# Turning the head outputs of the second half on VectorE, 32x32 blocks at a time, with the blocks moved by DMA

## The chip, the cores and the metric

The kernel runs on one core of a Trainium2 chip. The metric is the device time of one launch in microseconds (us). The core has five engines that run their own instruction streams and meet at semaphores: TensorE (PE, the matrix products, with its weight loads shown as PEld), VectorE (DVE), ScalarE (ACT), GpSimd (POOL) and SyncE (SP, which here only issues DMAs). On-chip memory (SBUF) has 128 partitions; PE writes into eight banks of PSUM, which DVE and ACT read.

## The reference

A hybrid encoder trunk of one layer over a sequence of 2048 tokens and 1024 features, in fp32:

```python
xn = rmsnorm(x, norm1_g[l])
z = xn @ w_in[l]
u_pool, zq, zf, zi, zo, zg = jnp.split(z, splits, axis=-1)
gates = jax.nn.sigmoid(zg + b_gate[l]).reshape(B, S, N_BRANCHES, D_MODEL)
ya = pool_mixer(u_pool, pool_w[l], pool_scale[l]) @ w_pa[l]
yb = hgrn2_mixer(zq, zf, zi, zo, lower_bounds[l], hgrn_norm_g[l]) @ w_pb[l]
merged = gates[:, :, 0] * ya + gates[:, :, 1] * yb
x = x + merged @ w_o[l]
x = x + conv_glu_ffn(rmsnorm(x, norm2_g[l]), w_up[l], conv_w[l], conv_b[l], w_down[l])
```

`hgrn2_mixer` is a gated linear recurrence with four heads of 128 features. What matters here is its end, where `o` is what the recurrence put out, `norm_g` a weight of 128 features that all heads share, and `zo` the output gate:

```python
o = o * lax.rsqrt(jnp.mean(o * o, axis=-1, keepdims=True) + EPS) * norm_g.astype(jnp.float32)
o = o * jax.nn.silu(heads(zo))
return o.reshape(B, S, HGRN_WIDTH).astype(zq.dtype)
```

The product with `w_pb` follows, which sums over the features.

## The kernel before

The sequence is cut into four blocks of 512 tokens (`TB`), and the program runs over two halves of two blocks: mixer (`mixer(b0)`, b0 = 0 and 2), then FFN. The large products are split into seven smaller ones (P1 to P7, in the manner of Strassen, on sums of quarters), and each is three matmuls in fp32r: every fp32 operand is a high part (a rounded copy, by ScalarE) and a low part (the difference, by VectorE). This is done by `split` (line 718 on, in the profile L724 and L725) for activations and by `Stream.convert` for the weights, whose rows in the profile are `ops<-raw` on ACT (L260) and DVE (L266). The weights are loaded by SP into eight buffers `raw` (`N_RAW`, L207) and turned into operands in six buffers `ops` (`N_OPS`).

The order is that of the code as it is written out, by generators: every sixth large matmul (`MM_PER_TICK`) calls `tick`, which advances the stream of weights and steps each open task; a task's `yield n` puts off its next piece by n ticks. All engines work through their own list in that order, as a scheduler in the framework lays it. `slots` is a pool of 73 SBUF buffers of 128x512 that all activations share, `banks` the eight PSUM banks: a tile that takes a buffer waits for the last reader of the tile before.

While the input projection runs (units `fr`, `gr` and others, seven products each, all of line 158 on PE), three runners (`N_RUN`) work through the eight pairs of block and head of the half (`hgrn_task(b, h, ...)`). Such a task starts when the projection has brought its `q` and `f` (L1316), goes through a chain of small DVE operations (L1175 to L1247) and PE products `pl` (L1155, L1227), the state (`pv`, `po`), and ends so:

- `ot` (L1295): four DVE operations, `po` by the reciprocal root and the output gate `z`; token on the partitions, feature along the row, 128 tokens in each of four pieces;
- four ticks later `pt` (L1301): four PE transposes of 128x128 fp32 into a bank, so that features come onto the partitions;
- `oh` (L1303): ScalarE copies the bank and multiplies by the norm's weight (`col(o_hg)`, one value for each partition);
- `spill` (L1120): ScalarE's queue stores the tile to a DRAM tile `od[b, h]` of 128x512, 256 KB.

Later in the same mixer, `o_task` fetches the eight tiles `od` into `oT` (SP, L1125), waits for a place in the program (`O_PLACE`), and splits each into `oTs` (high and low). These are the moving operands of the matmuls of `branch("pb", ...)`, the product with `w_pb` (`pb<-oTs_...` on PE), first for the lower block's chains, then for both in turn.

The first half (blocks 0 and 1) does the same.

Of the kernel before, what the change touches and what calls it, by code (L numbers as in the profile page):

```python
# [11 lines left out]
F32 = mybir.dt.float32  # L12
F32R = mybir.dt.float32r
U8 = mybir.dt.uint8
AF = mybir.ActivationFunctionType
ALU = mybir.AluOpType
AX = mybir.AxisListType

P = 128
# [3 lines left out]
HEADS = 4  # L23
# [6 lines left out]
TB = 512  # L30
NT = TB // P
SB = 1024
# [39 lines left out]
O_PLACE = 17  # L72
FIN_WAIT = 4
AHEAD = 3
GK = 32
NG = 4
ADD_LAG = 3
# [12 lines left out]
def tile_trunk(  # L90
# [17 lines left out]
    pe, act, dve, pool, sp = nc.tensor, nc.scalar, nc.vector, nc.gpsimd, nc.sync  # L108
# [7 lines left out]
    dram = ctx.enter_context(tc.tile_pool(name="dram", bufs=1, space=bass.MemoryType.DRAM))  # L116
    banks = ctx.enter_context(tc.tile_pool(name="banks", bufs=8, space=bass.MemoryType.PSUM))

    def slot(name, cols=TB, dt=F32):
        return slots.tile([P, cols], dt, tag="s", name=name, padded_shape=[P, 528])  # L120

    def bank(name, cols=512):
        return banks.tile([P, cols], F32, tag="b", name=name, padded_shape=[P, 512])

    def f32(ap):
        return ap.bitcast(F32)
# [513 lines left out]
    o_n1, o_n2, o_bg, o_ps, o_lb, o_hg, o_cb, o_cw = offs  # L640
# [8 lines left out]
    def col(o):  # L649
        return cols[:, o : o + 1]  # L650
# [19 lines left out]
    def setup_task():  # L670
# [8 lines left out]
        for key, x, off, w in keys:  # L679
# [8 lines left out]
                               channel_multiplier=-1)  # L688
            m8 = const.tile([P, GK // 2], U8, tag=f"m{key}", name=f"m{key}")
            yield 2  # L690
            for g in range(NG):
                r = slice(g * GK, g * GK + GK)
                pool.tensor_copy(m8[r], mf[r, g * GK // 2 : (g + 1) * GK // 2])
            masks[key] = m8.rearrange("p (b h) -> p b h", h=x)
        m8 = const.tile([P, GK], U8, tag="md", name="md")
        for g in range(NG):
            r = slice(g * GK, g * GK + GK)
            ins = pool.tensor_copy(m8[r], ident[r, r])
# [19 lines left out]
    def split(src, name, on_pool=False):  # L718
        hi = slot(name + "h", TB, F32R)
        lo = slot(name + "l", TB, F32R)  # L720
        if on_pool:
            up = pool.tensor_scalar(hi, src, 1.0, 0.0, ALU.mult, ALU.add)
        else:
            up = act.copy(hi, src)  # L724
        low = dve.tensor_tensor(lo, src, f32(hi), ALU.subtract)  # L725
        last_split[0] = up, low
        return hi, lo
# [395 lines left out]
    def fetch(d, name, eng=sp):  # L1123
        t = slot(name)
        eng.dma_start(t, d)  # L1125
        return t


    def hgrn_task(b, h, d, q, vd, zd, od):
        def head_of(src, key):  # L1130
            t = slot(f"{key}{b}_{h}")
            sp.dma_start(t.rearrange("p (c v) -> p c v", c=NT), src[:, :, h * P : (h + 1) * P])
            return t
# [8 lines left out]
        qv, dv, av = (t.rearrange("p (c x) -> p c x", c=NT) for t in (q, d, att))  # L1142
        ac = av[:, :, P - GK : P]

# [4 lines left out]
        def products(hh, qm):  # L1149
            x = GK // 2  # L1150
            pa_ = bank(f"pl{b}_{h}_{hh}", NT * 3 * x)
            ps = pa_.rearrange("p (c x) -> p c x", c=NT)
            for c in range(NT):
                for g in range(NG):
                    ins = pe.matmul(ps[g * GK : g * GK + GK, c],  # L1155
                                    ks[:, c * P + g * GK : c * P + g * GK + GK],
                                    qm[:, c, :, g * x : g * x + x], start=True, stop=True)
                    if not (c or g):
                        in_turn(ins)
            return ps  # L1160
# [16 lines left out]
        dve.tensor_tensor(qo, qm[:, :, 2], de, ALU.mult)  # L1177
        yield AHEAD
        ps = products(1, qm)
# [9 lines left out]
        for hh in (2, 8, 32):  # L1189
# [19 lines left out]
            dve.tensor_tensor(q2, f1, d5[:, :, :, 0, 0:1].to_broadcast(full), ALU.mult)  # L1209
            yield AHEAD  # L1210
            if hh < GK:
                x = GK // 2
# [80 lines left out]
        ot = slot(f"ot{b}_{h}")  # L1293
        for c in range(NT):
            dve.scalar_tensor_tensor(ot[:, c * P : (c + 1) * P], po[:, c * P : (c + 1) * P],  # L1295
                                     r[:, c : c + 1], zt[:, c * P : (c + 1) * P],
                                     ALU.mult, ALU.mult)
        yield 4
        pt = bank(f"pt{b}_{h}")
        for c in range(NT):  # L1300
            pe.transpose(pt[:, c * P : (c + 1) * P], ot[:, c * P : (c + 1) * P], ident)  # L1301
        t = slot(f"oh{b}_{h}")
# [131 lines left out]
    def add_forms(two, forms, k, name, store=lambda p, t: None, sums=True, pin=lambda i: None,  # L1434
                  eng=pool):

        def comb(p, x0, x1, op):
            if (p, k) in forms or x0 is None or x1 is None:
                return
            t = slot(f"{name}_{p}_{k}")  # L1440
            pin(eng.tensor_tensor(t, x0, x1, op))  # L1441
            forms[p, k] = t
            store(p, t)

        for p, at in (("P1", (1, 0)), ("P2", (1, 1)), ("P4", (0, 1))):
            if (p, k) not in forms and at in two:
                forms[p, k] = two[at]
                store(p, two[at])
        if not sums:
            return  # L1450
        comb("P7", two.get((1, 0)), two.get((0, 0)), ALU.subtract)
        comb("P5", two.get((0, 0)), two.get((0, 1)), ALU.subtract)
        comb("P6", forms.get(("P5", k)), two.get((1, 0)), ALU.subtract)
        comb("P3", forms.get(("P6", k)), two.get((1, 1)), ALU.add)
# [84 lines left out]
    def mixer(b0, forms, late):  # L1539
# [4 lines left out]
        md, od, gd = {}, {}, {}  # L1544
# [11 lines left out]
        def runner():  # L1556
            while taken[0] < 2 * HEADS:
                if queue:
                    taken[0] += 1
                    yield from hgrn_task(*queue.pop(0))  # L1560
                else:
                    yield 1
# [124 lines left out]
        oT = {}  # L1687
# [70 lines left out]
        def evac_b(m, hf, g, ps):  # L1758
            gated(g, hf, g, ps)
            dve.tensor_tensor(y[m, hf], y[m, hf], g, ALU.add)  # L1760
            if m >= KD // 2 and hf:
                k = m - KD // 2
                two = {(h, r): y[k + r * (KD // 2), h] for h in range(2) for r in range(2)}
                add_forms(two, yf, k, f"yf{b0}", eng=dve)

        def o_task():
            t = {}
            for hf in range(2):
                for g in range(HEADS):
                    while (b0 + hf, g) not in od:  # L1770
                        yield 1
                    t[hf, g] = fetch(od[b0 + hf, g], f"oT{b0 + hf}_{g}")
            while place[0] < O_PLACE:
                yield 1
            for hf in range(2):
                for g in range(HEADS):
                    oT[hf, g] = split(t[hf, g], f"oTs{b0 + hf}_{g}")
                    yield 2

        otask = []  # L1780
        for d in range(2):
            units = [Unit(f"pa{b0}_{2 * d + e}", "pa", emit_a(2 * d + e)) for e in range(2)]
            for p in ORDER:
                place[0] += 1
                if (d, p) == (1, "P1"):
                    otask.append(Task(o_task()))
                for s_, hf in {"P6": ((1, 1),), "P5": ((0, 0),), "P7": ((1, 0),),
                               "P2": ((0, 1),)}.get(p, ()):
                    for e in range(2):
                        gate(0, 2 * d + e + KD // 2 * s_, hf)  # L1790
                while len(pf[FORM[p]]) < 2:
                    place[0] += 1
                    mtask.step()
                w = stream.get("pa")
                for e in range(2):
                    units[e].products(p, pf, pf[FORM[p]], w[:, :, e * 256 : e * 256 + 256])
                    units[e].after(p)
                stream.used(1)
# [279 lines left out]
    for b in range(0, SEQ // TB, 2):  # L2078
        forms, task, late = nxt
        if b:  # L2080
            join(task)
        forms, task, late = mixer(b, forms, late)
        join(task)
        nxt = ffn(b, forms, late)
# [51 lines left out]
```

## Time and profile before

| what | value |
|---|---|
| device time, median of 3 runs | 2461.87 us (2461.87 to 2462.55) |
| the profiled execution's own time | 2461.48 us |
| its span in the trace | 2459.8 us |
| mean granted clock of PE | 0.999 |
| HBM read and written | 403.55 MB, 200.81 MB |
| PE transposes `pt` of all 16 pairs | 64, of which 32 in the second half |

The span is what the instructions of the core cover; the device time has 1.7 us around it. The projection of the second half, with the heads' tasks in it, lies from about 1380 to 1660 us, the `pa` and `pb` products of that half follow, and then `w_o` and the FFN. In a timeline, a row is start, duration, engine, line, operation, the tile written, the tiles read, shapes and count; what stands in brackets at its end is the idle time of that engine ahead of it and what ended it. Matmuls are pipelined, so a duration there is longer than the distance to the next one's start. In a row of waits stand the sum in us, the count and the longest.

### The profile page before, as it was taken

What the parts mean: (1) busy time and instruction counts of PE and PEld (TensorE: products, weight loads), DVE (VectorE), ACT (ScalarE), POOL (GpSimd) and SP (SyncE); (2) the same over time, 40 slices, a digit from 0 to 9 for tenths busy, and PEclk for the clock granted to TensorE, in tenths of its full rate; (3) what the DMA queues carried; (4) which work ended last, traced back from release to release, by engine and by line L of the source; (5) the groups of instructions that cost most, each with busy time, mean ns of one, the idle gap of its engine ahead of it and who ended that gap; (6) DMA issues with size and microseconds to landing.
All of it is one profiled execution on the core that took longest, in us unless ns stands there. A gap on an engine that the chain in (4) does not pass through costs nothing.

```text
span 2459.8 us, 37972 instructions
## 1 busy us (share of the span) xinstructions
PE 2439.1 (99%) x12624; PEld 1979.3 (80%) x12624; DVE 1903.0 (77%) x3294; ACT 1232.0 (50%) x2372; POOL 750.7 (31%) x1068
## 2 busy tenths in 40 slices
PE   9999999999999999999999999999999999999998
PEld 7887777788888888888888888888888888888887
DVE  7777776997998778876586667768889987878755
ACT  6545544435555445555544555542465554445534
POOL 4343353403354334451210101112033332335310
PEclk9999999999999999999999999999999999999999
DMA  8989888977888779899784443478333444447852
GB/s 283 312 218 277 237 220 238 329 221 245 206 251 242 225 226 240 269 364 321 237 285 153 136 127 122 154 237 306 112 129 129 150 156 134 145 144 260 306 165 99
DMA packets 272612, 529.29 MB, mean 215 GB/s; under 512 B 28640, under 2 KB 49248, under 8 KB 272096
## 3 DMA queue, kind: packets, MB, share of 16 engines
q1 hardware_dynamic: 204560, 348.47, 42.4%
q0 software_dynamic: 42880, 113.27, 18.1%
q10 hardware_dynamic: 24976, 65.13, 7.6%
q8 instruction: 99, 1.62, 0.3%
q14 instruction: 97, 0.79, 0.1%
HBM read 403.55 MB, written 200.81 MB: 246 GB/s over the span
## 4 chain that ended last, share of the span: by engine, by line
PE 92%; DVE 3%; DMA 2%; ACT 1%; issue 1%; POOL 0%; SPq 0%; ACTq 0%; DVEq 0%; POOLq 0%
PE dn_P L158 17%; PE up_Z L158 15%; PE up_X L158 10%; PE up_V L158 10%; PE wo_P L158 6%; PE gr_V L158 3%; PE pb L158 3%; PE gr_X L158 3%; PE io_Z L158 2%; PE io_V L158 2%; PE gr_W L158 2%; PE gr_Y L158 2%; PE fr_X L158 1%; PE gr_Z L158 1%; PE fr_V L158 1%; PE ur_X L158 1%
## 5 line engine op out<-in xcount | busy, mean ns | idle before, releaser
L260 ACT CAST ops<-raw 128x512 fp32r<-128x512 f32 x802 | 493.4, 620 | 784.8 <-PE dn_P L158 161.5
L266 DVE TENSOR_TENSOR ops<-raw,ops 128x512 fp32r<-128x512 f32 x774 | 571.4, 743 | 240.9 <-ACT ops L260 232.6
L1872 DVE SCALAR_TENSOR_TENSOR e<-h,cols,e 128x512 f32<-128x512 f32 x176 | 142.9, 817 | 30.3 <-ACT e L1870 26.9
L1870 ACT ACTIVATE e<-h,cols 128x512 f32<-128x512 f32 x176 | 142.2, 814 | 25.3 <-DVE h L1316 18.9
L1875 DVE SCALAR_TENSOR_TENSOR e<-h,cols,e 128x512 f32<-128x512 f32 x176 | 133.9, 770 | 2.5
L1125 POOL DMA_DIRECT2D g_P<-dg_P x154 | 83.0, 541 | 171.8 <-PE dn_P L158 133.0
L1441 POOL TENSOR_TENSOR gf_P<-e,e 128x512 f32<-128x512 f32 x44 | 61.1, 1390 | 149.5 <-DVE e L1881 85.8
L1441 POOL TENSOR_TENSOR gf_P<-gf_P,e 128x512 f32<-128x512 f32 x44 | 58.2, 1322 | 74.1 <-DVE e L1881 71.6
L501 POOL TENSOR_TENSOR raw<-raw,raw 128x512 f32<-128x512 f32 x32 | 46.5, 1453 | 90.7 <-DVE ops L266 81.8
L1879 ACT ACTIVATE e<-e 128x512 f32<-128x512 f32 x88 | 55.6, 632 | 36.6 <-DVE e L1875 36.4
L1865 POOL COPY h<-h 128x2 f32<-128x2 f32 x88 | 39.3, 459 | 106.6 <-DVE h L1315 103.8
L1316 DVE TENSOR_TENSOR h<-up_u,up_V 128x512 f32<-128x512 f32 x88 | 60.1, 683 | 10.5 <-PE up_V L158 10.0
L1867 POOL COPY hist<-h 128x2 f32<-128x2 f32 x88 | 35.2, 400 | 101.5 <-DVE h L1316 99.3
L1413 DVE TENSOR_TENSOR x<-x,wo_P 128x512 f32<-128x512 f32 x88 | 55.8, 678 | 11.8 <-PE wo_P L158 11.7
L1865 POOL COPY h<-hist 128x2 f32<-128x2 f32 x88 | 45.0, 517 | 55.4 <-DVE h L1316 25.1
L1581 POOL TENSOR_TENSOR q<-q,qs 128x512 f32<-128x512 f32 x16 | 22.3, 1393 | 119.2 <-ACT qs L1580 119.2
L1413 DVE TENSOR_TENSOR ac<-ac,dn_P 128x512 f32<-128x512 f32 x72 | 47.3, 681 | 11.5 <-PE dn_P L158 11.0
L1614 ACT ACTIVATE gt<-gt,cols 128x512 f32<-128x512 f32 x48 | 34.8, 724 | 42.5 <-DVE gt L1316 41.3
L1356 ACT COPY up_e<-up_X 128x512 f32<-128x512 f32 x44 | 25.8, 587 | 60.1 <-PE up_X L158 38.6
L1895 POOL DMA_DIRECT2D dg_P<-gf_P x88 | 50.7, 576 | 8.9 <-POOL gf_P L1441 7.2
L758 POOL TENSOR_SCALAR ro<-so 128x4 f32<-128x4 f32 x16 | 4.1, 256 | 151.3 <-ACT sq L1289 151.1
L1755 POOL TENSOR_TENSOR ya<-ya,gl 128x512 f32<-128x512 f32 x24 | 35.8, 1512 | 47.2 <-DVE ya L1752 39.6
(1335 smaller groups left out, 7855.2 us busy)
## 6 DMA issues: line engine op xcount, KB each, us to landing
g_P<-dg_P POOLq DMA_DIRECT2D x154, 256.0 KB, 5.9
raw<-in_w_up_t SPq DMA_DIRECT2D x132, 256.0 KB, 3.1
raw<-in_w_in_t SPq DMA_DIRECT2D x98, 256.0 KB, 3.7
dg_P<-gf_P POOLq DMA_DIRECT2D x88, 256.0 KB, 3.8
dg_P<-e SPq DMA_DIRECT2D x66, 256.0 KB, 3.2
raw<-in_w_dn SPq DMA_DIRECT2D x66, 256.0 KB, 5.4
x<-in_x SPq DMA_DIRECT2D x64, 256.0 KB, 5.2
gd<-gt ACTq DMA_DIRECT2D x64, 256.0 KB, 3.6
```

The lines of the kernel that those rows point to most:

```text
L158: count[1] = pe.matmul(*args, **kw)
L260: self.mark = act.copy(hi, v)
L266: low = self.low = dve.tensor_tensor(lo, v, f32(hi), ALU.subtract)
L1125: eng.dma_start(t, d)
L1316: return dve.tensor_tensor(dst, t, ps, ALU.add if how == "add" else ALU.subtract)
L1413: dve.tensor_tensor(t, t, ps[j], ALU.add if sg > 0 else ALU.subtract)
L1441: pin(eng.tensor_tensor(t, x0, x1, op))
L1865: pool.tensor_copy(h[:, 0:2], hist[:, mt] if hf == 0 else hs[s, 0][:, TB : TB + 2])
L1870: in_turn(act.activation(t, h[:, 2:], AF.Identity, bias=col(o_cb + mt), scale=col(o_cw + 4 * MF + mt)))
L1872: in_turn(second(dve.scalar_tensor_tensor(t, h[:, 1 : 1 + TB], col(o_cw + 2 * MF + mt), t, ALU.mult, ALU.add)))
L1875: dve.scalar_tensor_tensor(t, h[:, 0:TB], col(o_cw + mt), t, ALU.mult, ALU.add)
L1879: in_turn(act.activation(g, g, AF.Silu))
```

## The change

For blocks 2 and 3 and heads 0 to 2 (`BY_BLOCKS` = 3), six of the sixteen pairs, the PE transposes, the ScalarE copy and the store on ScalarE's queue are not issued. In their place DVE transposes `ot` in 32x32 blocks, in one instruction (`blocks_turned`, into a slot `oz`). Its output is written so that within a block the four pieces of 128 tokens stand side by side: the elements that follow each other in the transpose lie 16 bytes apart. Two ticks later `blocks_moved` has SP issue four DMAs, each of 32 partitions with four runs of 512 bytes (64 KB), which bring the blocks to their places in `od`. In `od` the order of the tokens along the row is then "m c" (token within a piece, then piece) and the norm's weight isn't in it. So `o_task` splits these six tiles by `split_turned`: ScalarE and DVE read `oT` with a step of four elements, multiply by the norm's weight (`activation` with scale, `scalar_tensor_tensor`), and write the high and low part in the usual order.

```diff
@@ -72,6 +72,7 @@
 O_PLACE = 17
 FIN_WAIT = 4
 AHEAD = 3
+BY_BLOCKS = HEADS - 1
 GK = 32
 NG = 4
 ADD_LAG = 3
@@ -1125,6 +1126,17 @@
         eng.dma_start(t, d)
         return t
 
+
+    def blocks_turned(t, name):
+        z = slot(name)
+        dve.transpose(z.rearrange("p (b j c) -> p b c j", b=4, c=NT),
+                      t.rearrange("p (c b i) -> p b c i", c=NT, b=4))
+        return z
+
+    def blocks_moved(dst, z, eng=sp):
+        d = dst.rearrange("(b i) (a m) -> a i b m", b=4, a=4)
+        for a in range(4):
+            eng.dma_start(d[a], z[32 * a : 32 * a + 32].rearrange("i (b m) -> i b m", b=4))
 
     def hgrn_task(b, h, d, q, vd, zd, od):
         def head_of(src, key):
@@ -1295,6 +1307,12 @@
             dve.scalar_tensor_tensor(ot[:, c * P : (c + 1) * P], po[:, c * P : (c + 1) * P],
                                      r[:, c : c + 1], zt[:, c * P : (c + 1) * P],
                                      ALU.mult, ALU.mult)
+        if b >= SB // TB and h < BY_BLOCKS:
+            oz = blocks_turned(ot, f"oz{b}_{h}")
+            yield 2
+            od[b, h] = dram.tile([P, TB], F32, tag=f"od{b}_{h}", name=f"od{b}_{h}")
+            blocks_moved(od[b, h], oz)
+            return
         yield 4
         pt = bank(f"pt{b}_{h}")
         for c in range(NT):
@@ -1763,6 +1781,14 @@
                 two = {(h, r): y[k + r * (KD // 2), h] for h in range(2) for r in range(2)}
                 add_forms(two, yf, k, f"yf{b0}", eng=dve)
 
+        def split_turned(t, name):
+            hi, lo = (slot(name + c, TB, F32R) for c in "hl")
+            v = t.rearrange("p (m c) -> p c m", c=NT)
+            h4, l4 = (x.rearrange("p (c m) -> p c m", c=NT) for x in (hi, lo))
+            act.activation(h4, v, AF.Copy, scale=col(o_hg))
+            dve.scalar_tensor_tensor(l4, v, col(o_hg), f32(h4), ALU.mult, ALU.subtract)
+            return hi, lo
+
         def o_task():
             t = {}
             for hf in range(2):
@@ -1774,7 +1800,8 @@
                 yield 1
             for hf in range(2):
                 for g in range(HEADS):
-                    oT[hf, g] = split(t[hf, g], f"oTs{b0 + hf}_{g}")
+                    part = split_turned if b0 and g < BY_BLOCKS else split
+                    oT[hf, g] = part(t[hf, g], f"oTs{b0 + hf}_{g}")
                     yield 2
 
         otask = []
```

The lines of the changed file stand 1 to 19 lower (L1301 becomes L1319, L1316 becomes L1334, L266 becomes L267, L1175 becomes L1187). What the change moves in the engines' lists is shown at three places. In the names, the number after the letter is the head, and the last one a serial number of the tile.

PE, in the projection, where head 0 of block 3 is turned, before and after (`gr` is a unit of the projection, `x_f0h` its input's high part, `ops` the weights):

```order
L158 MATMUL gr_1_X<-x_f0h,ops_14633 128x512
L158 MATMUL gr_1_X<-x_f1h,ops_14633 128x512
L1301 MATMUL pt_0_14789<-ident,ot_0_14720 128x128 x4
L158 MATMUL gr_1_X<-x_f1l,ops_14633 128x512
L158 MATMUL gr_1_X<-x_f1h,ops_14633 128x512
L158 MATMUL gr_1_X<-x_f2h,ops_14633 128x512
```

```order
L159 MATMUL gr_1_X<-x_f0h,ops_14633 128x512
L159 MATMUL gr_1_X<-x_f1h,ops_14633 128x512
L159 MATMUL gr_1_X<-x_f1l,ops_14633 128x512
L159 MATMUL gr_1_X<-x_f1h,ops_14633 128x512
L159 MATMUL gr_1_X<-x_f2h,ops_14633 128x512
```

The group of four is gone and its neighbours close up; the other five groups go in the same way, and the rest of PE's list differs only in where some `pl` products of the later heads stand among the projection's matmuls.

DVE at the same place (`p` and `s` belong to the pooling branch, `q` and `f` to head 1), before and after:

```order
L266 TENSOR_TENSOR ops_14706<-raw_14444,ops_14706 128x512
L1316 TENSOR_TENSOR q_1_14677<-fr_1_u_14675,fr_1_V 128x512
L266 TENSOR_TENSOR ops_14746<-raw_14477,ops_14746 128x512
L1295 SCALAR_TENSOR_TENSOR ot_0_14720<-po_0_14643,ro_0_14658,z_0_14584 128x128 x4
L1094 SCALAR_TENSOR_TENSOR p_1_14725<-s_1_2_14618,u_1_14491 128x512
L1316 TENSOR_TENSOR q_1_14737<-fr_1_u_14675,fr_1_Y 128x512
L266 TENSOR_TENSOR ops_14771<-raw_14500,ops_14771 128x512
L1094 SCALAR_TENSOR_TENSOR p_1_14751<-s_1_2_14665,u_1_14435 128x512
L1316 TENSOR_TENSOR f_1_14763<-fr_1_u_14606,fr_1_V 128x512
```

```order
L267 TENSOR_TENSOR ops_14713<-raw_14444,ops_14713 128x512
L1334 TENSOR_TENSOR q_1_14679<-fr_1_u_14677,fr_1_V 128x512
L1307 SCALAR_TENSOR_TENSOR ot_0_14718<-po_0_14645,ro_0_14660,z_0_14584 128x128 x4
L267 TENSOR_TENSOR ops_14746<-raw_14477,ops_14746 128x512
L1132 STREAM_TRANSPOSE oz_0_14723<-ot_0_14718 128x4x4x32
L1095 SCALAR_TENSOR_TENSOR p_1_14725<-s_1_2_14618,u_1_14491 128x512
L1334 TENSOR_TENSOR q_1_14737<-fr_1_u_14677,fr_1_Y 128x512
L267 TENSOR_TENSOR ops_14776<-raw_14500,ops_14776 128x512
L1095 SCALAR_TENSOR_TENSOR p_1_14756<-s_1_2_14667,u_1_14435 128x512
L1334 TENSOR_TENSOR f_1_14768<-fr_1_u_14606,fr_1_V 128x512
```

`ot` stands ahead of the weights' low part (`ops_14746`) now, and the transpose behind it. A little further in the same list, the operations of head 1 for the two blocks (q_1_14737 for the one, q_1_14677 or q_1_14679 for the other) stand in another order, before and after:

```order
L1204 TENSOR_TENSOR qm_1_2_14895<-q_1_14737,f_1_14699 128x4x16x2
L1243 TENSOR_TENSOR f_1_14699<-f_1_14699 128x64
L1241 TENSOR_TENSOR q_1_14737<-q_1_14737,f_1_14699 128x64x2
L1208 TENSOR_TENSOR qm_1_2_14895<-qm_1_2_14895,f_1_14699 128x4x64
L1209 TENSOR_TENSOR q_1_14737<-qm_1_2_14895,f_1_14699 128x64x4
L266 TENSOR_TENSOR ops_14880<-raw_14564,ops_14880 128x512
L1244 TENSOR_TENSOR f_1_14699<-f_1_14699 128x64
L1175 TENSOR_TENSOR qm_1_1_14805<-q_1_14677,f_1_14763 128x4x64
```

```order
L1216 TENSOR_TENSOR qm_1_2_14891<-q_1_14737,f_1_14706 128x4x16x2
L267 TENSOR_TENSOR ops_14876<-raw_14564,ops_14876 128x512
L1255 TENSOR_TENSOR f_1_14706<-f_1_14706 128x64
L1187 TENSOR_TENSOR qm_1_1_14801<-q_1_14679,f_1_14768 128x4x64
L1188 TENSOR_TENSOR q_1_14679<-q_1_14679,f_1_14768 128x256
L1253 TENSOR_TENSOR q_1_14737<-q_1_14737,f_1_14706 128x64x2
L1220 TENSOR_TENSOR qm_1_2_14891<-qm_1_2_14891,f_1_14706 128x4x64
```

The operand `qm_1_1` of the second block (L1175, now L1187) stands ahead of three operations of the first block (L1241, L1208 and L1209) that it stood behind, and of one that takes `f` further (L1244).

SP, from the weights' loads around head 0's stores, before and after:

```order
L207 DMA raw_14636<-kwg2ins_2594 128x512
L207 DMA raw_14689<-kwg2ins_2616 128x512
L207 DMA raw_14709<-kwg2ins_2708 128x512
L207 DMA raw_14749<-in_w_in_t 128x512
L207 DMA raw_14774<-in_w_in_t 128x512
```

```order
L208 DMA raw_14636<-kwg2ins_2594 128x512
L1139 DMA od_0_14693<-oz_0_14643 32x4x128 x2
L208 DMA raw_14691<-kwg2ins_2616 128x512
L1139 DMA od_0_14693<-oz_0_14643 32x4x128 x2
L208 DMA raw_14716<-kwg2ins_2708 128x512
L208 DMA raw_14749<-in_w_in_t 128x512
L1139 DMA od_0_14751<-oz_0_14723 32x4x128 x4
L208 DMA raw_14779<-in_w_in_t 128x512
```

The four stores of each block stand between loads of raw weights, so they go out in SP's order with them.

## The prediction

> **What bounds the kernel now.** I read the page's header and busy time first, then the chain of work that ended last, then the stretch in which the edited work lies.
>
> ```profile
> span 2459.8 us, 37972 instructions
> PE 2439.1 (99%) x12624; PEld 1979.3 (80%) x12624; DVE 1903.0 (77%) x3294; ACT 1232.0 (50%) x2372; POOL 750.7 (31%) x1068
> PE 92%; DVE 3%; DMA 2%; ACT 1%; issue 1%; POOL 0%; SPq 0%; ACTq 0%; DVEq 0%; POOLq 0%
> ```
>
> TensorE (PE) carries the end of the program; every other engine has room on average. An average hides stages, so next come the edited heads of blocks 2 and 3, 1380 to 1660 us. The columns are the window, its length, busy time of PE, PEld, DVE, ACT and POOL, the granted clock, the DMA share and GB/s.
>
> ```profile
> 1380.00:1660.00 280.00, 279.36 (x1989) 229.16 (x1988) 194.11 (x467) 140.63 (x330) 40.38 (x55) 1.00 0.48 157
> ```
>
> PE is busy for 279.36 of 280 us at full clock: a matmul taken out of this stretch shortens the run by the room it takes in PE's stream, unless something else is then late. The waits (who, for whom; us, count, longest) name candidates: the first row is PE's largest in this stretch, the second PE's for its pl products over the whole run, the last that of SyncE's queue (SP) here.
>
> ```profile
> PE pa_V L158 <- DVE ya L1752: 0.6, 1, 0.6
> ...
> PE pl L1155 <- ACT k L1138: 2.3, 3, 1.2
> ...
> SPq L207 <- DVE ops L266: 141.7, 53, 5.1
> ```
>
> The three waits of the pl row fall in the first half of the sequence: there the recurrence of a head was late for its pl products. In this stretch it is not.
>
> **Removed: 24 transposes on PE.** These rows are PE's timeline (start, us, operation) around the first and the last of the six groups that go, and the row that counts the groups of all eight blocks in this half.
>
> ```profile
> 1405.03 0.39 PE L158 MATMUL fr_Y<-x_T41h,ops 128*128 128x512 f32 x1
> 1405.26 0.60 PE L1301 MATMUL pt<-ident,ot 128*128 128x128 f32 x4
> ...
> 1405.93 0.39 PE L158 MATMUL fr_Y<-x_T41h,ops 128*128 128x512 f32 x1
> ...
> 1550.74 0.40 PE L158 MATMUL fr_X<-x_f1h,ops 128*128 128x512 f32 x1
> 1550.97 0.60 PE L1301 MATMUL pt<-ident,ot 128*128 128x128 f32 x4
> ...
> 1551.64 0.39 PE L158 MATMUL fr_X<-x_f1h,ops 128*128 128x512 f32 x1
> ```
>
> ```profile
> L1301 PE MATMUL pt<-ident,ot x32: 271/272/273, 1405.3 to 1641.5; 128*128 128x128 f32 x32
> ```
>
> Here I chose how to count. By the busy time of one transpose, 24 x 0.272 = 6.5 us would go. But matmuls overlap: the matmul at 1405.03 shows 0.39 and the next operation starts 0.23 later. So I take the pitch. From the matmul ahead of the group (1405.03) to the second one behind it (1405.93) are 0.90 us, where two matmuls alone would take 2 x 0.23 = 0.46: the group costs 0.44. The last one gives the same (1550.74 to 1551.64, 0.90); the other four show 0.90 or 0.91. **Six groups: 6 x 0.44 = 2.64 us.**
>
> *Skill against the row.* The Trainium skill, "VectorE: DVE Perf Modes", section "The three transpose paths", has TensorE at 390 ns and VectorE at 311 ns for a 128x128 bf16 transpose; its "Rules for kernel authors" prefer TensorE where a PSUM destination will do, which speaks against this change. By 390 ns the removal would be worth an estimated 9.4 us; the trace's pitch says a quarter of that, and its busy time of 272 ns does not agree with the page either.
>
> Also removed are six ScalarE copies with their scale (0.69 us each) and six stores issued by ScalarE. ACT is busy 140.63 of 280 and PE waits for it nowhere here: nothing gained.
>
> ```profile
> L1303 ACT ACTIVATE oh<-pt,cols x16: 667/686/690, 184.3 to 1641.8; 128x512 f32<-128x512 f32 x16
> L1120 ACTq DMA_DIRECT2D od<-oh x16: 326/326/554, 185.1 to 1642.5; - x16
> DMA to landing us min/median/max: 2.1/3.3/8.4
> ```
>
> **Added: six transposes on VectorE.** The trace has none. The nearest rows: a plain 128x512 operation takes 0.68 to 0.69 us; and operations whose elements lie apart cost more per element.
>
> ```profile
> L1243 DVE TENSOR_TENSOR f<-f 128x64 f32<-128x64 f32 x6 | 1.8, 294 | 0.1
> L1243 DVE TENSOR_TENSOR f<-f 128x4 f32<-128x4 f32 x6 | 0.9, 152 | 0.0
> ```
>
> At a step of 32 bytes L1243 takes (294 - 152) / 60 = 2.4 ns per element, where the plain operation takes at most 690 / 512 = 1.35. The new transpose reads in a row and writes at a step of 16 bytes. **Bounds: 0.69 us, and 0.15 + 512 x 2.4 ns = 1.4 us; I take 1.3**, nearer to L1243, since its step is nearer and the operation is no plain copy. (An estimate from the page cited above, 4 x 311 ns = 1.24 us, lies inside.) Above 1.4 no row speaks, so that is a rival below.
>
> Is there cover? VectorE (DVE) in head 0 of block 3, with the idle ahead of each row in brackets, and in the second fence PE's first pl products of head 1, of both blocks:
>
> ```profile
> 1405.67 0.69 DVE L266 TENSOR_TENSOR ops<-raw,ops 128x512 fp32r<-128x512 f32 x1 [1.96 <-ACT ops L260]
> 1406.28 1.12 DVE L1295 SCALAR_TENSOR_TENSOR ot<-po,ro,z 128x128 f32<-128x128 f32 x4
> ...
> 1410.53 0.69 DVE L1316 TENSOR_TENSOR f<-fr_u,fr_V 128x512 f32<-128x512 f32 x1 [0.74 <-PE fr_V L158]
> ...
> 1414.15 0.30 DVE L1241 TENSOR_TENSOR q<-q,f 128x128 f32<-128x128 f32 x1 [0.18 <-ACT qm L1199]
> ...
> 1415.17 0.68 DVE L266 TENSOR_TENSOR ops<-raw,ops 128x512 fp32r<-128x512 f32 x1
> ...
> 1415.96 0.42 DVE L1175 TENSOR_TENSOR qm<-q,f 128x256 f32<-128x256 f32 x1
> ```
>
> ```profile
> 1416.42 0.89 PE L1155 MATMUL pl<-qm,k 128*32 128x48 f32 x64
> ```
>
> By the new order, `ot` moves ahead of the `ops` at 1405.67, into its 1.96 us of idle, and the transpose takes the place at which `ot` stood. The second cover is the 0.74 idle ahead of `f` at 1410.53, of which 0.44 is gone, since PE delivers fr_V one group earlier. So a transpose of up to 1.12 + 0.30 = 1.42 us delays nothing; at 1.3 it is hidden. For the next head the idle ahead of the same operation is 1.44:
>
> ```profile
> 1480.36 0.69 DVE L1316 TENSOR_TENSOR f<-fr_u,fr_V 128x512 f32<-128x512 f32 x1 [1.44 <-PE fr_V L158]
> ```
>
> which covers 1.12 + 1.44 - 0.44, some 2.1 us. Behind the third pair the `f` of head 3 stands 24 rows later in the order, so it isn't delayed.
>
> **The tight place is pl.** By 1416 PE has lost both groups of the pair and is 0.88 us early. Before, the second block's `qm` (L1175) ended at 1416.38, and its half of pl began some 0.42 after 1416.42, at 1416.84: slack 0.46. In the new order the L1241 at 1414.15 and the two rows behind it stand after this L1175, which therefore comes 1415.17 - 1414.15 + 0.18 = 1.2 us earlier. Slack now: 0.46 + 1.2 - 0.88 = 0.78, less some 0.3 for a weight load and a semaphore: **0.5 us, no wait at the likeliest, but little to spare.** The next product of the chain (hh 2) comes out at 0.5 to 0.85 in the same way.
>
> **Moved: stores on SP.** Each 64 KB store becomes four, 24 instead of 6, and they stand on SP between the loads of raw weights instead of on ScalarE's queue. Four issues take 4 x 0.33 to 4 x 0.55 = 1.3 to 2.2 us (L1120's rows). SP stands 141.7 us of this stretch waiting for one of the eight raw buffers to come free, 53 times, 2.7 us on average, so the issues fall into waits it has anyway, and a load that goes out some 2 us late has seven older tiles ahead of it. Without that cover each store would hold PE up by what SP waits for its transpose, at most some 3 us. DVE operations that reuse a transpose's buffer now wait for these stores to land. In the order the reuse stands a whole head's tail later (the first store goes out by some 1400, its buffer is written after 1409), so at the median landing of 3.3 us they come 3 us or more ahead; at the 8.4 of the slowest row DVE would stand 2.5 us once, behind which wait `ops` and the chain of head 3, with some 2 us of idle to take it up: cost 0 to 0.5, taken as 0.
>
> **Changed: the split of o.** ScalarE and VectorE now read with a step of 16 bytes, multiply by the norm's weight and write in a row. The tight place is VectorE's last new low part, that of the second block's head 2, against PE's first use of it:
>
> ```profile
> 1682.26 1.77 DVE L725 TENSOR_TENSOR oTs_2l<-oT,oTs_2h 128x512 fp32r<-128x512 f32 x1
> ...
> 1687.35 0.39 PE L158 MATMUL pb<-oTs_2l,ops 128*128 128x512 f32 x1
> ```
>
> It ends at 1684.03 and is used at 1687.35: slack 3.3. If each of three low parts grows by 0.6 (some doubling, as at L1243) and the first high part, which ScalarE makes ahead of them, by as much, that is 2.4. Covered; bounds 0 and 0.5, taken 0.
>
> **Sum.** The profiled execution took 2461.48 us (span 2459.8), 0.39 below the median of 2461.87. 2461.48 - 2.64 = 2458.8; from the median, 2459.2. Forecast **2459.0**.
>
> **Rivals.**
> *Pl gives it back.* If my 0.5 us of slack is spent (a longer transpose, a slower semaphore), PE waits at the pl products of heads 1 and 2, as it does in the first half: 2.3 us in 3 waits, 1.2 the longest. For: the chain behind `f` is serial, and moves up by 0.44 while PE moves up by 0.88. Against: the new order pulls the late instruction forward by 1.2. Two to four waits of 0.4 to 1.0 give 1 to 2.6 back: 2460 to 2461.7.
>
> *Slower: the transpose is long.* If moving single elements across partitions costs far more than any row, each transpose beyond 1.42 us (first pair) or 2.1 (second) delays `f`, and beyond the slack of 0.5 PE. The saving of 2.64 is eaten when (T - 1.92) + (T - 2.6) = 2.64, at T = 3.6 us; at 4 us the time is 2462.3, at 6.2 us 2466.7, and from there the difference can be told. For: no row shows the operation. Against: 3.6 us is 7 ns per element, three times L1243's.
>
> *Faster: a transpose costs PE its busy time.* If the room that a group takes is more than the pitch shows, because the fp32 transposes hold PE in a way that the neighbours hide, 6.5 us go: 2455.0. Against: six groups with the same 0.90 between starts. By the Trainium skill's 390 ns, cited above, it would be 2452.1; no row bears that out.
>
> **How the numbers follow.** About 0.2% (4.9 us) is what a measurement of this kernel can tell from no change: below 2456.9 is faster, above 2466.8 slower. Forecast (2457.5 to 2460) 0.66; give-back 0.15; slower rival 0.13, of which 0.05 stay under 2466.8; faster rival 0.06. So faster 0.06, same 0.86, slower 0.08. The range, 2456.8 to 2464.0, takes in the forecast, the give-back and the nearer part of the slower rival and leaves out some 0.16.
>
> **What would show it.** Right: PE's row spacing around the places of the six groups is 0.23 throughout; the first-to-last time of 1380 to 1660 is shorter by 2.6; the transposes are rows of 0.7 to 1.4 us with no new idle before `f`; the pl rows of heads 1 and 2 show no wait over 0.2; oTs_2l ends before its use. Wrong: a wait of PE on `qm`, `k` or `ops` after 1405 that the old profile lacks, a transpose above 2 us, SP waiting on a transpose with the raw loads behind it late at PE, or spacing that shrinks by more than 0.44 at a group.

## The result and the profile after

The changed kernel takes **2456.27 us** (median of 15 runs, 2454.70 to 2458.91) where the kernel before takes 2461.87 (15 runs beside them, 2460.76 to 2464.08): a ratio of **0.9978**, 95% interval 0.9971 to 0.9985, or 5.4 us less (3.7 to 7.1). The forecast was 2459.0 with a range from 2456.8: the time lies below it by 0.5 us. The profiled execution took 2457.82 us.

The page of the changed kernel, header and busy time, and its window over the edited stretch (columns as for before):

```profile
span 2456.1 us, 37954 instructions
PE 2435.8 (99%) x12600; PEld 1977.2 (81%) x12600; DVE 1911.5 (78%) x3300; ACT 1231.9 (50%) x2366; POOL 756.6 (31%) x1068
...
1380.00:1660.00 280.00, 279.37 (x1976) 228.79 (x1976) 199.37 (x475) 137.89 (x326) 41.63 (x56) 1.00 0.50 160
```

PE has 24 operations less and is as busy as before in the stretch: the room was closed up, not left idle. Its timeline at the places of the first and the last group (line numbers are one higher or more now):

```profile
1406.47 0.39 PE L159 MATMUL fr_Y<-x_T41h,ops 128*128 128x512 f32 x1
1406.70 0.39 PE L159 MATMUL fr_Y<-x_T41l,ops 128*128 128x512 f32 x1
1406.93 0.39 PE L159 MATMUL fr_Y<-x_T41h,ops 128*128 128x512 f32 x1
...
1549.92 0.39 PE L159 MATMUL fr_X<-x_f1h,ops 128*128 128x512 f32 x1
1550.14 0.39 PE L159 MATMUL fr_X<-x_f1l,ops 128*128 128x512 f32 x1
1550.37 0.39 PE L159 MATMUL fr_X<-x_f1h,ops 128*128 128x512 f32 x1
```

From the first of these rows to the last are 143.90 us; the same two matmuls lay 1551.64 - 1405.03 = 146.61 apart. The six groups gave 2.71 us. That is the forecast's 2.64, and it isn't the whole gain. Laying each matmul of the changed kernel against the same matmul of before shows where the rest comes from:

| at (us in the trace of before) | changed kernel minus before (us) |
|---|---|
| 600 to 1404 | +1.44 |
| 1415, 1495, 1560 (behind groups 2, 4, 6) | +0.55, -0.33, -1.27 |
| 1660, 1740 | -1.23, -1.25 |
| 1850, 2000, 2100, 2230 | -1.53, -2.09, -2.62, -3.29 |
| 2300, the end of the span | -3.47, -3.68 |

The first row belongs to the opening, which differs from one execution to the next (below). The groups take off 2.7, and from 1740 to 2300 us another 2.2 go bit by bit, nearly all in the FFN of the second half, where the change edits nothing. Two matmuls near its ends show it, in the timeline of before and then of the changed kernel:

```profile
1831.73 0.39 PE L158 MATMUL up_Z<-m_T20h,ops 128*128 128x512 f32 x1
...
2227.46 0.39 PE L158 MATMUL up_Z<-m_T30h,ops 128*128 128x512 f32 x1
```

```profile
1830.22 0.39 PE L159 MATMUL up_Z<-m_T20h,ops 128*128 128x512 f32 x1
...
2224.20 0.39 PE L159 MATMUL up_Z<-m_T30h,ops 128*128 128x512 f32 x1
```

They lie 395.73 us apart before and 393.98 after, with the same instructions between them. The window from 1830 to 2230 us of before and of the changed kernel says that nobody waits there:

```profile
1830.00:2230.00 400.00, 400.00 (x1724) 323.49 (x1723) 334.43 (x474) 203.94 (x325) 137.86 (x219) 1.00 0.45 145
```

```profile
1830.00:2230.00 400.00, 400.00 (x1732) 324.52 (x1731) 336.06 (x476) 204.73 (x326) 139.28 (x220) 1.00 0.45 146
```

PE is busy for all of the 400 us at full clock in both, and does 1724 operations in the one and 1732 in the other: the same matmuls follow each other more closely. As a mean over that FFN's 1,848 matmuls, one starts 232.15 ns after the other before and 231.12 after: 1.9 of the 2.2 us, the rest lying in the w_o ahead of it and the down product behind. In the FFN of the first half both have 231.4.

### The profile page after: what moved, and what is told of

It is laid out like the page before. It is cut to its first block, busy times and chain, and to the rows that moved or that the text cites. A ratio compares the mean times of both kernels' runs of the same rounds, so it can differ in the third digit from the quotient of the medians.

```text
span 2456.1 us, 37954 instructions
## 1 busy us (share of the span) xinstructions
PE 2435.8 (99%) x12600; PEld 1977.2 (81%) x12600; DVE 1911.5 (78%) x3300; ACT 1231.9 (50%) x2366; POOL 756.6 (31%) x1068
## 4 chain that ended last, share of the span: by engine, by line
PE 80%; DVE 1%; DMA 1%; issue 0%; ACT 0%; SPq 0%; POOL 0%; ACTq 0%; DVEq 0%
PE dn_P L159 17%; PE up_Z L159 15%; PE up_X L159 10%; PE up_V L159 10%; PE wo_P L159 6%; PE pb L159 3%; PE gr_V L159 2%; PE gr_X L159 2%; PE io_Z L159 1%; PE gr_Z L159 1%; PE gr_Y L159 1%; PE gr_W L159 1%; PE fr_V L159 1%; PE io_V L159 1%; PE fr_X L159 1%; PE m_t L871 1%
## 5 line engine op out<-in xcount | busy, mean ns | idle before, releaser
L267 DVE TENSOR_TENSOR ops<-raw,ops 128x512 fp32r<-128x512 f32 x774 | 574.8, 747 | 237.9 <-ACT ops L261 228.0
L1334 DVE TENSOR_TENSOR h<-up_u,up_V 128x512 f32<-128x512 f32 x88 | 60.2, 684 | 10.1 <-PE up_V L159 9.6
```

The lines of the kernel that those rows point to most:

```text
L267: low = self.low = dve.tensor_tensor(lo, v, f32(hi), ALU.subtract)
L1334: return dve.tensor_tensor(dst, t, ps, ALU.add if how == "add" else ALU.subtract)
```

## The experiments

One table holds what was read from each run. "Groups" is the distance of the two matmuls around the six groups (146.61 before), "FFN 1" and "FFN 2" that of two matmuls near the ends of the FFN of the first and of the second half (the pair of FFN 1 stands 12 matmuls closer together, so the two columns aren't compared with each other). The traces place the matmul at 1405.03 of before anywhere from 1403.77 to 1407.81, though every kernel but e12 and e4 (by its first group) runs the same PE instructions up to there: the opening, up to 440 us, varies that much. So the parts are read from distances behind it, which repeat to 0.03 us, and medians carry about 2 us of uncertainty.

| run | median, ratio (95%) | groups | FFN 1 | FFN 2 |
|---|---|---|---|---|
| before (first trace) | 2461.87 | 146.61 | 391.57 | 395.73 |
| changed (first trace) | 2456.27, 0.9978 (0.9971 to 0.9985) | 143.89 | 391.57 | 393.98 |
| e1 before again | 2460.54, 0.9997 (0.9988 to 1.0006) | 146.61 | 391.55 | 395.72 |
| e2 changed again | 2456.29, 0.9976 (0.9967 to 0.9985) | 143.89 | 391.56 | 393.99 |
| e3 no transposes | 2459.53, 0.9989 (0.9980 to 0.9998) | 145.86 | 391.54 | 394.74 |
| e4 both transposes | 2460.26, 0.9995 (0.9986 to 1.0004) | see text | 391.57 | 395.10 |
| e5 banks only | 2461.67, 1.0001 (0.9992 to 1.0011) | 146.61 | 391.55 | 395.72 |
| e6 slots only | 2459.19, 0.9993 (0.9984 to 1.0002) | 146.61 | 391.54 | 394.64 |
| e7 transposed twice | 2457.82, 0.9985 (0.9976 to 0.9994) | 144.13 | 391.54 | 395.11 |
| e8 four heads | 2455.45, 0.9976 (0.9968 to 0.9985) | 143.89 | 391.55 | 393.62 |
| e9 changed, one slot | 2457.80, 0.9983 (0.9974 to 0.9992) | 143.89 | 391.55 | 395.02 |
| e10 changed, two slots | 2457.80, 0.9984 (0.9975 to 0.9993) | 143.89 | 391.55 | 395.89 |
| e11 four heads, one slot | 2456.45, 0.9981 (0.9972 to 0.9989) | 143.89 | 391.55 | 395.02 |
| e12 all sixteen pairs | 2460.30, 0.9996 (0.9987 to 1.0005) | 143.80 | 391.82 | 395.50 |
| e13 two tiles exchanged | one execution, 2460.90 | 146.61 | 391.57 | 395.48 |
| e14 four tiles exchanged | one execution, 2460.21 | 146.61 | 391.57 | 395.46 |

### The same two kernels again: is it the program?

> The kernel before, unchanged, beside itself on one chip: ratio 1.000. What is asked is its trace. In the first trace of before, TensorE's 512-column matmuls of the FFN of the second half (1800 to 2230 us) start 232.2 ns apart, and 231.05 ns apart in the trace of the changed kernel; that alone is 2.4 us between the two. Theory 'layout' (the pitch hangs on where tiles lie in this program): 232.2 ns again. Theory 'execution' (the pitch is that of one chip or one execution): another value, and not tied to the program.

> The changed kernel once more, on the same chip as the other runs of this call. Ratio about 0.9977 (5.6 us). Theory 'layout': the FFN of the second half starts its matmuls 231.05 ns apart again, and the six places of the groups give 2.6 us. Theory 'execution': the pitch there is that of before on this chip, and the 5.6 us must lie elsewhere. Theory 'full price' (a transpose costs PE 0.23 to 0.27 us each, and one trace hid it): the places of the groups give 5.5 to 6.5 us.

Both came out as "layout" says. On one chip, in executions of their own, before has 395.72 us in FFN 2 and the changed kernel 393.99, each within 0.01 of its first trace. The distance belongs to the program. "Full price" fell here too: the groups give 2.72 again.

### Parts of the change

> Before, but the 24 transposes of heads 0 to 2 in blocks 2 and 3 are left out: ScalarE copies ot itself, so these heads' outputs aren't turned; all else, the stores on ScalarE's queue too, is as before. Its PSUM banks in the FFN of the second half are those of the changed kernel, its SBUF slots mostly those of before. Theory '0.44 per group and layout by banks': 2.6 us at the groups and 2.4 in the FFN, 5.0 to 5.8 in all, ratio 0.9978. Theory '0.44 per group and nothing else from the banks': 2.6 us, 0.9989. Theory 'full price': 5.5 to 6.5 at the groups.

```diff
-        pt = bank(f"pt{b}_{h}")
-        for c in range(NT):
-            pe.transpose(pt[:, c * P : (c + 1) * P], ot[:, c * P : (c + 1) * P], ident)
+        if b >= SB // TB and h < HEADS - 1:
+            pt = ot
+        else:
+            pt = bank(f"pt{b}_{h}")
...
```

The median, 2.6 us less, looks like the forecast, and the trace says that this is a coincidence: the stretch of the groups shrank by only 0.75, and FFN 2 by 1.0. PE's waits from 1360 to 1800 us of this kernel, and the row of the first of them with its idle time:

```profile
PE pl L1155 <- ACT k L1138: 1.5, 2, 0.8
PE pa_V L158 <- DVE ya L1755: 0.6, 1, 0.6
...
1416.76 0.55 PE L1155 MATMUL pl<-qm,k 128*32 128x48 f32 x32 [0.76 <-ACT k L1138]
```

The place is the one that the first rival of the prediction named, the second block's pl products of heads 1 and 2, and two waits of 0.76 are of the size that it gave. The engine is another. The prediction went by VectorE's `qm`; here are the second block's `qm` in e3, then ScalarE's rows up to `k` in e3 and in the changed kernel:

```profile
1415.39 0.43 DVE L1175 TENSOR_TENSOR qm<-q,f 128x256 f32<-128x256 f32 x1
```

```profile
1414.51 0.85 ACT L1137 ACTIVATE f<-f,lbt 128x512 f32<-128x512 f32 x1
1415.55 0.62 ACT L260 CAST ops<-raw 128x512 fp32r<-128x512 f32 x1 [0.20 <-PE gr_Z L158]
1416.08 0.63 ACT L1138 ACTIVATE k<-f 128x512 f32<-128x512 f32 x1
```

```profile
1414.44 0.61 ACT L261 CAST ops<-raw 128x512 fp32r<-128x512 f32 x1
1414.96 0.81 ACT L1149 ACTIVATE f<-f,lbt 128x512 f32<-128x512 f32 x1
...
1416.23 0.63 ACT L1150 ACTIVATE k<-f 128x512 f32<-128x512 f32 x1
```

In e3, `qm` was ready at 1415.82, 0.9 us before PE went on at 1416.76, and `k` only at 1416.71 (for head 2: 1485.73, 1486.68 and 1486.62). ScalarE's list in e3 has an `ops` that waits for PE between `f` and `k`. In the changed kernel an `ops` stands ahead of `f` and none between `f` and `k`, and `k` ends at 1416.86, 0.57 us before its half of pl (1416.99 + 0.44). e3 also keeps ScalarE's six copies and stores, which the change leaves out. So the 2.0 us that e3 gives back are due to ScalarE's list; whether to its order or to the copies in it, no run here separates.

> The changed kernel, with the 24 PE transposes of before put back beside VectorE's (their bank is read by nobody): the added parts of the change stand alone, and the banks of the FFN fall in a third way. Theory '0.44 per group': 2.6 us longer than the changed kernel at the groups. If layout sets the pitch of the FFN, that stage shows 231.0 or 232.2 ns, or a third value, by its banks: total 2458.9 or 2461.3. Theory 'full price': 2461.8 to 2462.8 with the pitch of the changed kernel.

```diff
             oz = blocks_turned(ot, f"oz{b}_{h}")
             yield 2
+            pt = bank(f"pt{b}_{h}")
+            for c in range(NT):
+                pe.transpose(pt[:, c * P : (c + 1) * P], ot[:, c * P : (c + 1) * P], ident)
```

The first group stands two ticks earlier here, ahead of the first marked matmul, so the stretch is read from 1380 to 1600 us: the difference to before is +0.04 us at its start and +0.03 at its end. The added parts (VectorE's transposes, 24 stores on SP, the reordered lists) cost nothing, and the transposes on PE all of the 2.7. FFN 2 showed a third value, 395.10.

> The changed kernel with each of VectorE's six transposes done twice, 2.2 us in place of 1.1. Theory 'cover' (up to 1.42 us hidden at heads 0 and 1, 2.1 behind, and 0.5 of slack at pl): PE waits some 0.3 us for each pair's first pl products at head 1, nothing at head 2; the stretch from 1404 to 1560 us gains 2.1 to 2.7 on before, where the changed kernel gains 2.7. Theory 'tight': every transpose beyond the first delays pl by its 1.1, and the gain of the stretch falls to 0.5 or less. The FFN's operands lie in a further layout, so its pitch is told apart.

```diff
             oz = blocks_turned(ot, f"oz{b}_{h}")
+            dve.transpose(oz.rearrange("p (b j c) -> p b c j", b=4, c=NT),
+                          ot.rearrange("p (c b i) -> p b c i", c=NT, b=4))
```

"Cover" held: 144.13, a gain of 2.48 where 2.1 to 2.7 were forecast, 0.24 less than in the changed kernel, and no row of pl among PE's waits. The scheduler laid VectorE's list anew for the second transpose, so this is the cover with a list made for it.

> The changed kernel with head 3 done in the same way (eight of the sixteen pairs). Theory '0.44 per group': two more groups, 0.88 us more by 1660 us, 3.5 in all against before, with no pl product behind them to wait; the fourth tile's split adds 1 us to VectorE's work ahead of pb, where 3.3 us are spare, so no wait on oTs. Theory 'full price': 1.8 to 2.2 us more. Rival: VectorE's low parts now end after PE's use and PE waits 0.5 to 2 us for oTs_3l. The FFN has 51 of 56 operands in other slots, so its pitch may lie anywhere from 231.0 to 232.2 or a little beyond: total 0.9985 to 0.9975 of before.

(`BY_BLOCKS = HEADS`.) The difference to before goes from +0.92 at 1404 us to -2.62 at 1660: 3.54 us for eight groups, as 0.44 per group says, with no wait for oTs. FFN 2 is the shortest seen, 393.62. It is no faster than the changed kernel by a measurable amount (0.9976 beside 0.9976 and 0.9978).

> All sixteen pairs turned on VectorE, in the first half too. Theory '0.44 per group and pl': eight more groups, 3.5 us, go in the first half, but PE waits there at pl already (4.4 us in all, the bound being the recurrence's chain on VectorE, ScalarE and GpSimd), so of the 3.5 at most 1.5 come through and the transposes may add waits: the first half gains between -2 and +2 us. The FFN of the first half has 47 of 56 operands in other slots and its pitch, 231.4 in all runs so far, changes. Rival: the gain is whole, 7 us in all at the groups, ratio 0.996.

(`BY_BLOCKS = HEADS`, and the conditions on `b` and `b0` taken out.) The ratio is 0.9996. PE's waits up to 620 us have rows that before lacks, or has smaller (gr_V by gt 0.6, pb by oTs_2l 0.3):

```profile
PE pl L1167 <- ACT qm L1186: 2.5, 1, 2.5
PE gr_V L159 <- DVE gt L1334: 2.2, 1, 2.2
...
PE pb L159 <- DVE oTs_1l L1789: 1.1, 1, 1.1
PE pb L159 <- DVE oTs_2l L1789: 1.0, 1, 1.0
```

Against before it is 4.4 us ahead by 360 us, has lost 2.6 of that by 420 at pl and gr_V, and loses 2.5 more by 600, where the slower split of o is late for pb (2.6 us in three waits). So nothing of the first half's gain is left.

### Banks or slots

> Before, with one more PSUM bank taken (one DVE memset of one column) ahead of the second half's w_o product, so that the banks of the FFN behind it fall in another order, while every operand of its matmuls lies in SBUF where it lay before. Theory 'slots' (the pitch of the FFN's matmuls hangs on where their moving operands lie in SBUF): 232.2 ns as before, ratio 1.000. Theory 'banks' (it hangs on the PSUM banks): another pitch, down to 231.0 ns, and up to 2.3 us less, ratio 0.9991.

> Before, with one more SBUF slot taken (one GpSimd memset of one column) at the same place, so that 26 of the 56 operand tiles of the FFN of the second half lie in other slots; the PSUM banks, the weights' buffers and the orders of the engines' instructions are as before. Theory 'slots': the pitch there leaves 232.2 ns (which way isn't known; the values seen so far are 231.0, 231.4, 231.5, 231.7 and 232.2), by up to 2.3 us in the run, and every stage ahead of it keeps its times. Theory 'banks': 232.2 ns, no change.

```diff
         branch("pb", 1, oT, evac_b, each_b)
         quiet[0] = False
+        if b0:
+            dve.memset(bank("spare")[:, :1], 0.0)                 # e5
+            pool.memset(slot("spare0")[:, :1], 0.0)               # e6
```

(One of the two lines in each.) The marked matmuls of the second FFN, banks only and then slots only:

```profile
1831.18 0.39 PE L158 MATMUL up_Z<-m_T20h,ops 128*128 128x512 f32 x1
...
2226.89 0.39 PE L158 MATMUL up_Z<-m_T30h,ops 128*128 128x512 f32 x1
```

```profile
1830.82 0.39 PE L158 MATMUL up_Z<-m_T20h,ops 128*128 128x512 f32 x1
...
2225.46 0.39 PE L158 MATMUL up_Z<-m_T30h,ops 128*128 128x512 f32 x1
```

395.71 with other banks, as before; 394.64 with other slots. Banks are out, slots it is.

> The changed kernel with one more SBUF slot taken ahead of the second half's w_o (as in the run of slots alone), so that 28 of the 56 operand tiles of the FFN lie elsewhere and nothing else moves. Theory 'slots': the FFN of the second half leaves 231.03 ns, and the run's shift against the changed kernel is that difference times about 1,950 matmul starts, to 0.1 us; the stretch of the groups keeps its 2.7 us. Rival (the change itself, not the layout, speeds the FFN): 231.0 ns and the time of the changed kernel.

> The same with two more slots taken (30 of 56 operand tiles elsewhere). Theory 'slots': a further pitch between some 230.8 and 232.3 ns, and the run's length follows it. Rival: 231.0 ns.

> All four heads of the second half turned on VectorE, with one more slot taken ahead of w_o. The stretch to 1660 us as in the run of four heads (3.5 us less than before); the FFN's pitch, 230.9 ns there, takes another value, likely higher, since 230.9 is the lowest seen; total 0.9975 to 0.9985 of before.

The same lines added to the changed kernel (one slot, two slots) and to e8 (one). The groups keep 143.89 in all three, and FFN 2 takes 395.02, 395.89 and 395.02. With e10's slots, the FFN between its marks is slower than before's, and what remains is what the change itself is worth: a difference of -0.12 us to before ahead of the groups and -2.83 behind them. Against the changed kernel FFN 2 is 1.04 us longer in e9 and 1.91 in e10, and both medians 1.5 us higher: they follow, but not to the 0.1 us that I expected, which the scatter of the opening doesn't allow. None of these lines makes a faster kernel.

### Which tiles

> Before, with the SBUF slots of two operand tiles of the second half's FFN exchanged, the high and low part of B221 (by one GpSimd memset of one column of the low part ahead of the split); all other tiles and banks lie as before. Theory 'each tile by its place' (the pitch of a product is set by its own operands' slots): the 12 matmuls with B22 operands leave 232.0 ns, all other products keep theirs, and the 395.73 us between the two marked matmuls move by no more than 0.5. Theory 'whole set' (something common to the stage, like which slots other engines use, sets the pitch): nothing moves, or all products move together.

> Before, with the slots of T33's high and low part exchanged in the same way, and, as the pool hands on what came free, those of T42's low and T43's high part. Theory 'each tile by its place': the products with T3 and T4 operands leave 232.9 and 232.2 ns, the others keep theirs or follow only where they come behind these. Theory 'whole set': nothing moves, or all move together.

```diff
         lo = slot(name + "l", TB, F32R)
+        if name == "m3_B221":      # e14: "m3_T33"
+            pool.memset(f32(lo)[:, :1], 0.0)
```

The marked matmuls of e13 in its timeline:

```profile
1831.06 0.39 PE L158 MATMUL up_Z<-m_T20h,ops 128*128 128x512 f32 x1
...
2226.54 0.39 PE L158 MATMUL up_Z<-m_T30h,ops 128*128 128x512 f32 x1
```

395.48: a quarter of a microsecond for two tiles of 256 KB that changed places. Mean distance of matmul starts, by the operand set that the product reads, from all starts of that FFN:

| operand set | before | e1 | e13 | e14 |
|---|---|---|---|---|
| f | 231.97 | 231.97 | 231.97 | 231.82 |
| T2 | 232.12 | 232.12 | 232.11 | 232.11 |
| T1 | 232.00 | 232.01 | 232.00 | 232.06 |
| T3 | 232.85 | 232.84 | 232.84 | 232.61 |
| T4 | 232.17 | 232.13 | 232.10 | 231.60 |
| B22 | 231.99 | 232.00 | **231.15** | 232.00 |

In e13 only the product with the exchanged tiles moves. In e14 the two with exchanged tiles move, and a little the set f, whose tiles kept their slots; f and T1 stand right behind T3 and T4 in PE's order, and single starts of both moved there by several ns. So a product's pace follows the slots of its own moving operands first; that those of the product ahead of it matter a little too is what e14 suggests, and no run tests it.

## Why the prediction was wrong

- **What bounds the kernel: right.** PE stayed at 279.37 of 280 us in the stretch, and what went out of its stream came off the end.
- **Removed, 6 x 0.44 = 2.64 us: right.** 2.71 to 2.72 in both traces, 3.54 for eight groups. The rival of 6.5 us by busy time is out: the pitch of the stream, not the row's duration, prices a matmul among others.
- **Added, 1.3 us per transpose: near.** The rows of the changed kernel:

```profile
L1139 SPq DMA_DIRECT2D od<-oz x24: 302/424/1506, 1399.8 to 1548.0; - x24
L1132 DVE STREAM_TRANSPOSE oz<-ot x6: 1085/1102/1141, 1398.7 to 1545.0; 128x512 f32<-128x512 f32 x6
...
DMA to landing us min/median/max: 1.6/2.1/4.8
```

1.10 us, inside 0.69 to 1.4. This is 276 ns per 128x128, fp32. The Trainium skill, "VectorE: DVE Perf Modes", section "The three transpose paths", has 311 ns in bf16; its order (VectorE below TensorE) says nothing of the gain here, since on PE the price was 0.11 us per transpose.
- **Cover and pl: no wait, as forecast, but the slack belongs to another operand.** VectorE's list and then PE's:

```profile
1407.72 1.08 DVE L1132 STREAM_TRANSPOSE oz<-ot 128x512 f32<-128x512 f32 x1
...
1411.53 0.69 DVE L1334 TENSOR_TENSOR f<-fr_u,fr_V 128x512 f32<-128x512 f32 x1 [0.42 <-PE fr_V L159]
...
1415.93 0.40 DVE L1187 TENSOR_TENSOR qm<-q,f 128x256 f32<-128x256 f32 x1
```

```profile
1416.99 0.89 PE L1167 MATMUL pl<-qm,k 128*32 128x48 f32 x64
```

`f` still waits for PE (0.42 of idle, where the forecast's 0.74 less 0.44 leaves 0.30), and `qm` ends at 1416.33, 1.1 us before the second block's half of pl (1416.99 + 0.44), where 0.5 to 0.78 were forecast. But the operand that comes last there is ScalarE's `k`, 0.57 us ahead of its use (0.48 for head 2). The prediction left it out, though the row of pl that it shows names `k` (the first half's rows of pl, by `k` and by VectorE's `qm`, add up to 4.4 us, not 2.3). That its 0.5 fits is luck. Of the 0.3 that it took off for a weight load and a semaphore, e3 shows 0.05 between the end of `k` and PE's start. It also put the end of ScalarE's copies at nothing gained; in e3, which keeps them, PE waits for ScalarE, so that they are worth nothing isn't shown.
- **Moved to SP: right.** SP waits 6.5 us for six transposes and PE for no weight: PE's only wait from 1360 to 1800 us is the one that it had.

```profile
SPq L1139 <- DVE oz L1132: 6.5, 6, 2.4
```

```profile
PE pa_V L159 <- DVE ya L1770: 0.6, 1, 0.6
```

- **Split of o: covered, as forecast.** The rows of the high part, of the last new low part, and of its use:

```profile
L1788 ACT ACTIVATE oTs_2h<-oT,cols 128x512 fp32r<-128x512 f32 x2 | 2.4, 1214 | 0.0
...
1683.06 1.13 DVE L1789 SCALAR_TENSOR_TENSOR oTs_2l<-oT,cols,oTs_2h 128x512 fp32r<-128x512 f32 x1
...
1686.65 0.39 PE L159 MATMUL pb<-oTs_2l,ops 128*128 128x512 f32 x1
```

ScalarE's part doubled, 0.62 to 1.21 us, and VectorE's shorter rows grew from 0.68 to 1.13 (in both kernels some take longer, as the 1.77 that the prediction shows, or 2.18 for oTs_1l after; why isn't shown); 2.5 us remain. The Trainium skill, "SBUF — State Buffer", section "Door 1: The DMA port swizzle", has 16-byte lines with a penalty for each crossing into another; a read at a step of 16 bytes agrees, which takes 1.21 us where ScalarE's same operation on elements in a row took 0.71 (e3, `oh<-ot`). In the first half (e12) the same growth makes PE wait.
- **The sum: here it failed.** "2461.48 - 2.64" took every stage outside the edited one to keep its time, and no rival had a mechanism that acts elsewhere without a wait. The missing term is -2.2 us. Of this, 1.9 lie in the up product of the second FFN: by taking other buffers in another order, the change handed other slots to 17 of the 56 operand tiles of that stage (by the addresses in the two built programs). The remaining 0.3, in the w_o ahead and the down product behind, are not traced to a cause. Neither its size nor its sign could have been worked out from the trace of before; that there may be such a term could, as the order of the pool's buffers changes, the stage is PE's own, and the same products start 231.4 ns apart in the first FFN and 232.15 in the second. That the change fell on a faster layout is luck: with two more slots taken (e10), its FFN 2 is slower than before's. Of the range, the lower bound was therefore too near: over the thirteen layouts of FFN 2 that were run the marked distance went from 393.62 to 395.89, and before's 395.73 is the second slowest of them, so another layout was likely to be faster, which nobody knew. The rest up to the median (5.6 against 2.7 + 2.2) is within the interval, and the opening varies more than that.

## What to carry to other kernels

Price a matmul in a full PE stream by the distance between starts with and without it, and look for the tightest chain that PE then reaches earlier. Look at every operand of that chain and at the new order of every engine that makes one: in e3 an operand of ScalarE's held the gain at 0.75 us instead of 2.7, with VectorE's ready. And where a change alters which buffers a pool hands out, lay the two traces against each other matmul by matmul before crediting the edit: 2.2 of the 4.9 us found in the trace came from stages that it didn't touch, and one spare slot (e9) took more than half of those 2.2 away again.

## What the runs showed of the hardware that was not expected

PE's pace in a stage that never waits depends on where its moving operands lie in SBUF: 230.9 (e8) to 232.15 ns (before) between starts of 128x512 fp32r matmuls as means over one FFN, 229.7 to 234.2 for single operand sets (e8's T4, e10's T2), the same to 0.04 ns in two executions of one program, unmoved by other PSUM banks (395.71 against 395.73), and set product by product (e13: 231.99 to 231.15 for the product whose two tiles were exchanged, all others within 0.07; in e14 the products behind the exchanged ones moved a little too). Which property of the addresses decides it stays open: neither the address of a tile nor its distance to the next one, by any power of two up to 64 KB, sorted the starts of five layouts.
